# Seven-product matrix blocks: P3 ahead of P6, with P6's right block made by an accumulating DMA

## The chip, the core and the metric

The kernel runs on one core of a Trainium2 chip. The metric is the device time of one execution in microseconds. Five engines work side by side, each through its own queue in program order: TensorE (PE) multiplies and accumulates into banks of PSUM, VectorE (DVE) and ScalarE (ACT) do elementwise work and empty those banks, GpSimd (POOL) and SyncE (SP) here mostly issue DMAs. PE's weight loads are shown as an engine of their own (PEld).

## The reference

A trunk of two layers over 512 positions of width 1024, in float32. Each layer is half a SwiGLU mixer, a token mixer, and half a SwiGLU mixer again; layer 0 mixes tokens with a gated linear recurrence, layer 1 with a chunked spatial gate.

```python
def swiglu(x, w_in, w_out):
    g, u = jnp.split(x @ w_in, 2, axis=-1)
    return (jax.nn.silu(g) * u) @ w_out

for i in range(DEPTH):
    h = h + 0.5 * swiglu(rms_norm(h, ffn1_norm[i]), ffn1_w_in[i], ffn1_w_out[i])
    hn = rms_norm(h, mix_norm[i])
    ...
    h = h + m
    h = h + 0.5 * swiglu(rms_norm(h, ffn2_norm[i]), ffn2_w_in[i], ffn2_w_out[i])
return rms_norm(h, final_norm)
```

`w_in` is 1024 x 5632 and `w_out` 2816 x 1024 for each of the four SwiGLU mixers; the token mixers have a 1024 x 2048 input matrix and a 1024 x 1024 output matrix. Weights are read from device memory once or more; the work is almost wholly matrix products.

## The kernel before

**Precision.** Every float32 operand is split into a high and a low half of type fp32r: ACT rounds the value (`hi`, `whi`), DVE subtracts it from the original (`lo`, `wlo`). A product is three matmuls of 128x512 (lines 345 to 347): high by high, low by high, high by low.

**Seven products for eight.** A pair of 2x2 block matrices, left A and right B, is multiplied with seven block products (Winograd's form). The left sums are S1 = A21 - A22, S2 = S1 - A11, S4 = S2 + A12 and S3 = -S2 - A22. The products are taken in the order of `ORDER` (line 46):

| product | left (`LEFT`) | right | PSUM bank (`BANK`) |
|---|---|---|---|
| P1 | A11 | B11 | A, cleared |
| P2 | A12 | B21 | B, cleared |
| P5 | S1 | B11 + B12 | C, cleared |
| P6 | S2 | B11 + B12 + B22 | A, added to |
| P3 | S4 | B22 | C, added to |
| P7 | S3 | B12 + B22 | A, added to |
| Q4 | A22 | B11 + B12 + B21 + B22 | A, added to (`Q` of its own in output blocks) |

Each bank name stands for two PSUM banks, one for each of two halves `s` of the rows. Right after a product its `posts` entry reads the bank: it takes what has been summed in it so far, and the next product on that bank goes on adding to it. The post is ACT's or DVE's.

**Steps.** A product is done in two halves of its inner dimension, `ci` = 0 and 1, so one set of seven is 14 steps, each with a right block of 512 KB (two 128x512 tiles side by side) and 12 matmuls. In four of the output sets the first half is only one tile wide (256 KB, 6 matmuls). The main loop (line 1357) writes out, for step i: hooks of phase `pre`; the sum of step i+4, if it has one (`Sub.add`, line 1364); the split of step i+3 (`SPLIT_AHEAD`; `Sub.split`, ACT's `whi` and then DVE's `wlo`); hooks of phases `mid` and `rest`; new loads; the matmuls of step i, with the posts behind each row half. What is written out first stands first in an engine's queue. `whi` and `wlo` have four buffers each (line 59), so the split of step i+3 takes the buffers of step i-1 and cannot begin before that step's matmuls are done.

**Right blocks.** A `Raw` (line 111) is a weight block in one of eight buffers; SP loads it as soon as a buffer is free. Sums of weight blocks are made in two ways. `Raw.add` (line 136) issues a DMA from POOL's queue that adds another block from device memory onto the tile. `Sub.add` (line 163) sums two tiles on DVE and may then start an accumulating DMA onto the second tile (`tile_then`). `Sub.split` starts an accumulating DMA onto the tile it has just split, if the block has a `then` (line 184).

**Where sets stand.** `chunk` (line 624) makes 512 columns of gate and up products of a SwiGLU mixer, 20 sets in all; `out_blocks` (line 530) multiplies with `w_out` and adds into the residual `X`, 14 sets (one for each token mixer, three for each SwiGLU mixer, of which the first has the short first half); `seven_chunk` (line 1020) is one set in the spatial mixer. That is 35 sets, 70 halves. In a chunk the posts of P1, P5, P6 and P7 are ACT copies (`c<-A`, `c<-C`), those of P2 and P3 DVE operations. In an output set all posts are DVE's `upd` (line 545, `x<-A`, `x<-B`, `x<-C`). The token mixers' output sets do P1, P2, P5 of the first half, then of the second, then the rest product by product.

**Left sums.** `sums` (line 609) puts S2, S4 and S3 (DVE) on three successive steps; `Group.parts` splits them (`hi` on ACT, `lo` on DVE), in an output set at a place fixed by the product's position in the order (line 591). `BlockNorm.rest` does the same after a normalisation.

Of the kernel before, what the change touches and what calls it, by code (L numbers as in the profile page):

```python
# [11 lines left out]
ALU = mybir.AluOpType  # L12
# [30 lines left out]

ORDER = ("P1", "P2", "P5", "P6", "P3", "P7", "Q4")
LEFT = {"P1": "A11", "P2": "A12", "P5": "S1", "P6": "S2", "P3": "S4", "P7": "S3", "Q4": "A22"}
BANK = {"P1": ("A", True), "P2": ("B", True), "P5": ("C", True), "P6": ("A", False), "P3": ("C", False),
        "P7": ("A", False), "Q4": ("A", False)}
# [3 lines left out]
def trunk(ctx: ExitStack, tc: tile.TileContext, a: dict, out: bass.AP):  # L53
# [32 lines left out]
    def tt(o, x, y, op):  # L86
        nc.vector.tensor_tensor(out=o, in0=x, in1=y, op=op)  # L87
# [120 lines left out]
    def hook(n, phase, fn):  # L208


        hooks.setdefault((n, phase), []).append(fn)
# [106 lines left out]
    def seven(block, cuts, left, w, posts, order=None, own=False, apart=False, joined=None):  # L318

        bk, raw, held = {}, {}, []
        banks = dict(BANK, Q4=("Q", True)) if apart else BANK

        def mm_of(prod, ci):
            name, fresh = banks[prod]
            pairs = cuts[ci]

            def mm(sub):
                if fresh and ci == 0:
                    for s in range(2):
                        bk[name, s] = bank(name)[:, :w]
                if prod == joined and ci == 0:
                    held.extend((sub, q, i) for q, i in enumerate(pairs))
                    return
                for s in range(2):
                    ps = bk[name, s]
                    k = {} if fresh else dict(skip_group_check=True)  # L340
                    for sb, q, i in (held if prod == joined else []) + [(sub, q, i) for q, i in enumerate(pairs)]:
                        zh, zl = left(prod, i, s)
                        wh, wl = sb.hi[:, q, :], sb.lo[:, q, :]
                        end = i == cuts[-1][-1]
                        nc.tensor.matmul(ps, zh, wh, start=fresh and i == 0, stop=False, **k)  # L345
                        nc.tensor.matmul(ps, zl, wh, start=False, stop=False, **k)  # L346
                        nc.tensor.matmul(ps, zh, wl, start=False, stop=end, **k)  # L347
                    if ci == len(cuts) - 1 and prod in posts:
                        posts[prod](s, ps)
            return mm  # L350

        order = order or [(p, ci) for p in ORDER for ci in range(len(cuts))]
        for prod, ci in order:
            def new(k, n, plus=None):
                b = lambda k, n: block(k, n, cuts[ci])
                return raw_of(b(k, n), [P, len(cuts[ci]), w], plus and b(*plus))

            tile = then = tile_then = None
            if prod == "P1":
                r = raw[11, ci] = new(0, 0)  # L360
            elif prod == "P2":
                r = new(1, 0)
            elif prod == "P5":
                if own:
                    raw[11, ci] = new(0, 0, (0, 1))
                else:
                    tile = raw[12, ci] = new(0, 1)
                    tile_then = block(1, 1, cuts[ci])
                r = raw[11, ci]
            elif prod == "P6":  # L370
                r, tile, then = raw[11, ci], new(1, 1), block(1, 0, cuts[ci])
                raw[22, ci] = tile
            elif prod == "P3":
                r = raw[22, ci]
            elif prod == "P7":
                r = new(0, 1, (1, 1)) if own else raw[12, ci]
            else:
                r = raw[11, ci]
            subs.append(Sub(r, mm_of(prod, ci), None, tile, then, tile_then))
        return order  # L380
# [49 lines left out]
    class BlockNorm:  # L430
# [21 lines left out]
        def rest(self, n, a22=4):  # L452

            for i, g in enumerate(self.g):
                if a22 is not None:
                    hook(n + (9 if self.plain else a22), "mid", lambda g=g: g.parts("A22"))
                hook(n + 4 + i, "pre", g.s2)
                hook(n + 5 + i, "mid", lambda g=g: g.parts("S2"))
                n4, n3 = (n + 6 + i, n + 8 + i) if self.plain else (n + 7 + 2 * i, n + 10 + i)
                hook(n4, "pre", g.s4)  # L460
                hook(n4 + 1, "mid", lambda g=g: g.parts("S4", True))
                if self.plain:
                    hook(n3, "pre", lambda g=g: tt(g.new("A21"), g.f["S1"], g.f["A22"], ALU.add))
                    hook(n3 + 2, "mid", lambda g=g: g.parts("A21", True))
                hook(n3, "pre", g.s3)
                hook(n3 + 1, "mid", lambda g=g: (g.parts("S3", True), g.f.pop("S2")))
                hook(n3 + 1, "late", lambda g=g: g.f.pop("A22"))
# [62 lines left out]
    def out_blocks(w, k0, groups, scale, norm=None, order=None, own=False):  # L530

        n = [g for g in groups]
        cuts, bases, i, r = [], {}, 0, k0
# [11 lines left out]
        def upd(t, c, src, sc):  # L545
            stt(xt(t, c), src, sc, xt(t, c), ALU.mult, ALU.add)
# [15 lines left out]
        def p5(s, ps):  # L562
            upd(2 + s, 1, ps, scale)

        def p6(s, ps):
            upd(s, 1, ps, -scale)

        def p3(s, ps):
            upd(s, 1, ps, scale)
            final(s, 1, "A12", s)  # L570

        def p7(s, ps):
# [33 lines left out]
            g.stage(n + 1, "A21", src(0, 2))  # L606
            sums(g, n + 3)

    def sums(g, n):
        for i, fn in enumerate((g.s2, g.s4, g.s3)):  # L610
            hook(n + i, "pre", fn)

    def in_block(w, col, cw):
# [10 lines left out]
    def chunk(w_in, f0, nt, group):  # L624
# [18 lines left out]
        def p5(s, ps):  # L643
            act(new(c5, s, "c5"), ps, AF.Copy)

        def p6(s, ps):
            act(new(c2, s, "c2"), ps, AF.Copy)

        def p3(s, ps):
            tt(c2[s], ps, c2[s], ALU.subtract)  # L650
            stt(c2[s], c2[s], rt(s), c1[s], ALU.mult, ALU.mult)
            ht[s] = c2[s]
            if s == 1:
                left_blocks(group, ht, 0)
# [158 lines left out]
    def recurrent(w_in, w_out, norm):  # L813
# [169 lines left out]
        for c in range(KD):  # L983
            mk(c * P, lambda ps, c=c: y_post(c, ps), False)
        order = [(p, ci) for ci in range(2) for p in ("P1", "P2", "P5")]
        order += [(p, ci) for p in ("P6", "P3", "P7", "Q4") for ci in range(2)]
        gs = out_blocks(w_out, 0, [2, 2], 1.0, norm, order, own=True)
        gs.update(enumerate(groups))

# [1 line left out]
    def spatial(w_in, w_out, norm):  # L991
# [28 lines left out]
        def seven_chunk(base, done):  # L1020
# [11 lines left out]
                tt(c1[s], c1[s], ps, ALU.add)  # L1032
                soon(2 + s, s, 0, c1[s], c1[s])

            def p3(s, ps):
                tt(c2[s], ps, c2[s], ALU.subtract)
                soon(3 + s, s, 1, c2[s], c2[s])

            def p7(s, ps):
# [4 lines left out]
            def q4(s, ps):  # L1044
# [1 line left out]

            seven(in_block(w_in, lambda n: base + n * 512, 512), [[0, 1], [2, 3]], x_left(), 512,
                  dict(P1=lambda s, ps: copy(c1, s, ps, "c1"), P2=p2, P5=lambda s, ps: copy(c5, s, ps, "c5"),
                       P6=lambda s, ps: copy(c2, s, ps, "c2"), P3=p3, P7=p7, Q4=q4), own=True)

        def v_done(t, n, o, src):
            v[t, n] = o
# [116 lines left out]
        groups[1].stage(u0 + 9, "A12", lambda q, s: hts[1][s][:, (2 + q) * P : (3 + q) * P])  # L1169
        groups[1].stage(u0 + 10, "A22", lambda q, s: hts[1][2 + s][:, (2 + q) * P : (3 + q) * P], None, False)  # L1170
        groups[1].stage(u0 + 11, "A21", lambda q, s: hts[1][2 + s][:, q * P : (q + 1) * P])
        sums(groups[1], u0 + 13)
        order = [(p, ci) for ci in range(2) for p in ("P1", "P2", "P5")]
        order += [(p, ci) for p in ("P6", "P3", "P7", "Q4") for ci in range(2)]
        gs = out_blocks(w_out, 0, [2, 2], 1.0, norm, order, own=True)
        gs.update(enumerate(groups))

# [222 lines left out]
```

## Time and profile before

| what | value |
|---|---|
| median of three runs | 1653.03 us (1652.65 to 1653.19) |
| profiled execution | 1654.62 us, span 1652.9 us |
| PE busy | 1624.5 us, 98% of the span |
| DVE busy | 1373.8 us, 83% |
| ACT busy | 1034.6 us, 63% |
| POOL busy | 210.5 us, 13% |
| DMA traffic | 271.97 MB |

The profile is of one execution. "Busy" is the time in which an engine has an instruction under way; matmuls overlap in their pipeline, so their starts tell more than their durations. A row of the timeline has the start in us from the beginning of the span, the duration in us, engine, line of the kernel, operation, and the tiles out<-in with buffer numbers left out; in brackets stands idle time of the engine before it and what ended it. A window row has a stretch, its length, the busy time of each engine in it with instruction counts, the TensorE clock that was granted, the share of the DMA engines and GB/s. A row of DMA issues ends with the size and the median us from issue to landing.

### The profile page before, as it was taken

The numbers are of one execution on the slowest core, as the hardware profiler recorded it, in microseconds if no ns is written. First come the engines' busy times: TensorE is split into PE (matmuls) and PEld (weight loads), VectorE is DVE, ScalarE is ACT, GpSimd is POOL, SyncE is SP. The second block draws the span as 40 slices with busy tenths as digits, with TensorE's granted clock in tenths as the row PEclk, the third lists the DMA queues.
The fourth block names the chain that finished last, engine by engine and source line by source line (L and its number), as shares of the span: only waits on it lengthen the run. The fifth ranks groups of instructions, "written<-read, shape, count | busy, mean of one in ns | idle before, by whom it ended". The sixth has DMA issues, their size and how long they took to land.

```text
span 1652.9 us, 20807 instructions
## 1 busy us (share of the span) xinstructions
PE 1624.5 (98%) x7475; PEld 1336.9 (81%) x7475; DVE 1373.8 (83%) x1825; ACT 1034.6 (63%) x1487; POOL 210.5 (13%) x191
## 2 busy tenths in 40 slices
PE   8999999989999999999999999999999999999996
PEld 6788888878878888888888888888888888888885
DVE  5898897786798897887988978878966988879777
ACT  6656656666867656556676565566874765665655
POOL 1111111200010111111101111111200011121110
PEclk9999999999999999999999999999999999999998
DMA  6767876952463866976838778768863557696683
GB/s 205 158 174 175 208 165 153 218 140 77 102 148 92 195 164 162 217 182 155 203 96 182 173 163 208 185 161 202 218 172 90 151 119 188 166 209 168 157 206 77
DMA packets 160744, 271.97 MB, mean 165 GB/s; under 512 B 11280, under 2 KB 37504, under 8 KB 160640
## 3 DMA queue, kind: packets, MB, share of 16 engines
q1 hardware_dynamic: 113424, 181.95, 36.0%
q0 software_dynamic: 44992, 86.06, 31.1%
q10 hardware_dynamic: 2224, 2.63, 0.5%
q8 instruction: 59, 0.97, 0.2%
q14 instruction: 45, 0.37, 0.1%
HBM read 268.50 MB, written 2.10 MB: 164 GB/s over the span
## 4 chain that ended last, share of the span: by engine, by line
PE 86%; DVE 8%; ACT 4%; issue 2%; DMA 1%; SPq 0%; ACTq 0%; DVEq 0%
PE A L346 13%; PE A L347 13%; PE A L345 13%; PE C L346 7%; PE C L347 7%; PE C L345 7%; PE B L345 3%; PE B L347 3%; PE B L346 3%; PE e L260 3%; DVE wlo L87 2%; PE p L694 1%; PE p L692 1%; PE p L693 1%; PE Q L347 1%
## 5 line engine op out<-in xcount | busy, mean ns | idle before, releaser
L96 ACT ACTIVATE whi<-raw 128x1024 fp32r<-128x1024 f32 (+1 forms) x539 | 556.4, 1034 | 421.4 <-PE A L346 107.4
L87 DVE TENSOR_TENSOR wlo<-raw,whi 128x1024 fp32r<-128x1024 f32 (+1 forms) x539 | 640.5, 1191 | 198.3 <-ACT whi L96 197.4
L345 PE MATMUL A<-whi,hi 128*128 128x512 f32 x984 | 393.0, 399 | 0.0
L346 PE MATMUL A<-whi,lo 128*128 128x512 f32 x984 | 385.5, 392 | 2.5 <-DVE lo L87 2.4
L347 PE MATMUL A<-wlo,hi 128*128 128x512 f32 x984 | 385.5, 392 | 0.2 <-DVE wlo L87 0.2
L346 PEld LDWEIGHTS A<-whi,lo 128*128 128x128 f32 x984 | 185.8, 189 | 41.7 <-DVE lo L87 4.8
L347 PEld LDWEIGHTS A<-wlo,hi 128*128 128x128 f32 x984 | 185.4, 188 | 40.8 <-DVE wlo L87 0.6
L345 PEld LDWEIGHTS A<-whi,hi 128*128 128x128 f32 x984 | 185.7, 189 | 36.5
L346 PE MATMUL C<-whi,lo 128*128 128x512 f32 x544 | 212.4, 390 | 0.9 <-DVE lo L87 0.7
L345 PE MATMUL C<-whi,hi 128*128 128x512 f32 x544 | 212.3, 390 | 0.0
L347 PE MATMUL C<-wlo,hi 128*128 128x512 f32 x544 | 211.8, 389 | 0.0
L136 POOL DMA_DIRECT2D raw<-in_ffn_w_in_dram x80 | 96.4, 1205 | 757.4 <-DVE raw L87 591.2
L87 DVE TENSOR_TENSOR raw<-raw,raw 128x1024 f32<-128x1024 f32 (+1 forms) x118 | 141.6, 1200 | 0.5
L87 DVE TENSOR_TENSOR lo<-a,hi 128x512 fp32r<-128x512 f32 (+1 forms) x196 | 127.8, 659 | 11.2 <-ACT hi L96 10.9
L136 POOL DMA_DIRECT2D raw<-in_ffn_w_out_dram x72 | 83.0, 1153 | 385.0 <-DMA raw<-in_ffn_w_out_dram 137.0
L346 PEld LDWEIGHTS C<-whi,lo 128*128 128x128 f32 x544 | 102.1, 188 | 24.1 <-DVE lo L87 3.2
L96 ACT ACTIVATE hi<-a 128x512 fp32r<-128x512 f32 (+1 forms) x196 | 117.4, 601 | 6.2 <-DVE a L87 4.0
L345 PEld LDWEIGHTS C<-whi,hi 128*128 128x128 f32 x544 | 102.1, 188 | 21.5 <-ACT c L96 0.4
L347 PEld LDWEIGHTS C<-wlo,hi 128*128 128x128 f32 x544 | 102.1, 188 | 21.0
L96 ACT ACTIVATE c<-A 128x512 f32<-128x512 f32 x126 | 74.1, 595 | 56.6 <-PE A L347 56.2
L345 PE MATMUL B<-whi,hi 128*128 128x512 f32 x272 | 109.2, 401 | 0.0
L347 PE MATMUL B<-wlo,hi 128*128 128x512 f32 x272 | 106.3, 391 | 0.0
(165 smaller groups left out, 2193.4 us busy)
## 6 DMA issues: line engine op xcount, KB each, us to landing
raw<-in_ffn_w_in_dram SPq DMA_DIRECT2D x160, 512.0 KB, 4.5
raw<-in_ffn_w_out_dram SPq DMA_DIRECT2D x100, 512.0 KB, 5.4
raw<-in_ffn_w_in_dram POOLq DMA_DIRECT2D x80, 512.0 KB, 7.6
raw<-in_ffn_w_out_dram POOLq DMA_DIRECT2D x60, 512.0 KB, 7.9
raw<-in_sg_w_in_dram SPq DMA_DIRECT2D x18, 512.0 KB, 5.0
raw<-in_rec_w_in_dram SPq DMA_DIRECT2D x16, 512.0 KB, 3.9
raw<-in_ffn_w_in_dram SPq DMA_DIRECT2D x30, 256.0 KB, 3.9
raw<-in_ffn_w_out_dram SPq DMA_DIRECT2D x20, 256.0 KB, 4.1
```

Of the source, the lines that this page charges most:

```text
L87: nc.vector.tensor_tensor(out=o, in0=x, in1=y, op=op)
L96: nc.scalar.activation(out=o, in_=x, func=f, **k)
L136: nc.gpsimd.dma_start(out=self.v, in_=src, accum_op=ALU.add)
L260: nc.tensor.transpose(ps[:, o : o + P], src(q, s), ident)
L345: nc.tensor.matmul(ps, zh, wh, start=fresh and i == 0, stop=False, **k)
L346: nc.tensor.matmul(ps, zl, wh, start=False, stop=False, **k)
L347: nc.tensor.matmul(ps, zh, wl, start=False, stop=end, **k)
L692: nc.tensor.matmul(ps, zh, wh, start=start and q == 0, stop=False)
L693: nc.tensor.matmul(ps, zl, wh, start=False, stop=False)
L694: nc.tensor.matmul(ps, zh, wl, start=False, stop=stop and q == 1)
```

## The change

P3 now stands ahead of P6 in all 35 sets. P6's right block B11 + B12 + B22 is no longer summed on DVE from P5's tile and a loaded B22: when P5's tile (B11 + B12) has been split, an accumulating DMA from POOL's queue adds B22 to it. B22 is still loaded for P3. In all, 70 DVE sums of 128x1024 leave, and 70 accumulating DMAs come; the number of plain loads, of matmuls and of ACT instructions is the same. Q4's block still gets its last term, B21, from an accumulating DMA after P6's split, which now stands two steps later. The banks keep their products, so P3 adds to C right after P5, and P7 adds to A right after P6. The posts of the two products are exchanged with them (c2 = P3, then c2 - P6), and S4 is made earlier and split ahead of S2's split.

```diff
-ORDER = ("P1", "P2", "P5", "P6", "P3", "P7", "Q4")
+ORDER = ("P1", "P2", "P5", "P3", "P6", "P7", "Q4")
...
                     tile_then = block(1, 1, cuts[ci])
-                r = raw[11, ci]
+                r, then = raw[11, ci], block(1, 1, cuts[ci])
             elif prod == "P6":
-                r, tile, then = raw[11, ci], new(1, 1), block(1, 0, cuts[ci])
-                raw[22, ci] = tile
+                r, then = raw[11, ci], block(1, 0, cuts[ci])
             elif prod == "P3":
-                r = raw[22, ci]
+                r = new(1, 1)
...
-                hook(n + 5 + i, "mid", lambda g=g: g.parts("S2"))
-                n4, n3 = (n + 6 + i, n + 8 + i) if self.plain else (n + 7 + 2 * i, n + 10 + i)
+                n4, n2, n3 = (n + 5 + i, n + 7 + i, n + 8 + i) if self.plain else (n + 6 + i, n + 8 + 2 * i, n + 10 + i)
+                hook(n2, "mid", lambda g=g: g.parts("S2"))
...
+        def p3(s, ps):
+            upd(s, 1, ps, scale)
+
         def p6(s, ps):
             upd(s, 1, ps, -scale)
-
-        def p3(s, ps):
-            upd(s, 1, ps, scale)
             final(s, 1, "A12", s)
...
-    def sums(g, n):
-        for i, fn in enumerate((g.s2, g.s4, g.s3)):
+    def sums(g, n, after=(0, 1, 2)):
+        for i, fn in zip(after, (g.s2, g.s4, g.s3)):
             hook(n + i, "pre", fn)
...
+        def p3(s, ps):
+            act(new(c2, s, "c2"), ps, AF.Copy)
+
         def p6(s, ps):
-            act(new(c2, s, "c2"), ps, AF.Copy)
-
-        def p3(s, ps):
-            tt(c2[s], ps, c2[s], ALU.subtract)
+            tt(c2[s], c2[s], ps, ALU.subtract)
             stt(c2[s], c2[s], rt(s), c1[s], ALU.mult, ALU.mult)
...
-        order += [(p, ci) for p in ("P6", "P3", "P7", "Q4") for ci in range(2)]
+        order += [(p, ci) for p in ("P3", "P6", "P7", "Q4") for ci in range(2)]
...
-            def p3(s, ps):
-                tt(c2[s], ps, c2[s], ALU.subtract)
+            def p6(s, ps):
+                tt(c2[s], c2[s], ps, ALU.subtract)
                 soon(3 + s, s, 1, c2[s], c2[s])
...
-                       P6=lambda s, ps: copy(c2, s, ps, "c2"), P3=p3, P7=p7, Q4=q4), own=True)
+                       P3=lambda s, ps: copy(c2, s, ps, "c2"), P6=p6, P7=p7, Q4=q4), own=True)
...
-        sums(groups[1], u0 + 13)
+        sums(groups[1], u0 + 13, (0, 0, 1))
```

More of the change, by code (lines that the diff above doesn't have):

```diff
@@ L1171, in spatial @@
         groups[1].stage(u0 + 11, "A21", lambda q, s: hts[1][2 + s][:, q * P : (q + 1) * P])
-        sums(groups[1], u0 + 13)
+        sums(groups[1], u0 + 13, (0, 0, 1))
         order = [(p, ci) for ci in range(2) for p in ("P1", "P2", "P5")]
-        order += [(p, ci) for p in ("P6", "P3", "P7", "Q4") for ci in range(2)]
+        order += [(p, ci) for p in ("P3", "P6", "P7", "Q4") for ci in range(2)]
         gs = out_blocks(w_out, 0, [2, 2], 1.0, norm, order, own=True)
```

## The prediction

> **What bounds the kernel now.** I read the page first: shares of the engines, DMA queues, the costly groups. Then the windows, to see where PE is idle at all.
>
> ```profile
> PE 1624.5 (98%) x7475; PEld 1336.9 (81%) x7475; DVE 1373.8 (83%) x1825; ACT 1034.6 (63%) x1487; POOL 210.5 (13%) x191
> ...
> q1 hardware_dynamic: 113424, 181.95, 36.0%
> q0 software_dynamic: 44992, 86.06, 31.1%
> ...
> L87 DVE TENSOR_TENSOR raw<-raw,raw 128x1024 f32<-128x1024 f32 (+1 forms) x118 | 141.6, 1200 | 0.5
> ```
>
> ```profile
> 0.00:150.00 150.00, 143.34 (x622) 113.42 (x623) 120.24 (x183) 92.86 (x145) 21.32 (x29) 0.98 0.71 183
> 150.00:300.00 150.00, 150.00 (x682) 124.03 (x681) 125.40 (x166) 88.12 (x110) 24.84 (x23) 1.00 0.75 176
> 300.00:450.00 150.00, 144.79 (x736) 122.27 (x735) 116.98 (x169) 105.69 (x164) 8.42 (x7) 0.99 0.50 123
> 1500.00:1653.00 153.00, 139.33 (x628) 114.57 (x626) 123.40 (x167) 86.25 (x121) 16.87 (x14) 0.97 0.63 152
> ```
>
> PE is the bound: 28.4 us of the span of 1652.9 are without a matmul, and 6.7, 5.2 and 13.7 of them lie in the three stretches with the opening, the first stage border and the tail. Elsewhere PE hardly stops. So the change can win a few us, and can lose wherever it makes PE wait. It touches PE in one way: each PSUM bank must have been read by the post of one product before the next product may add to it. Before, P5 (bank C) was followed by P6 on A, and P3 came back to C two steps later; P6 (A) was followed by P3 on C, and P7 came back to A two steps later. Now P5 and P3 stand back to back on C, and P6 and P7 on A. What decides is how soon the posts come.
>
> The next rows are the timeline around the border after P5 in a chunk: PE's last matmul on C and first on A, ACT's queue, DVE's split of P5's first half, POOL's two transfers onto P7's tiles. Behind them stand DMA rows of short windows: the first of these two transfers, the second, and P6's two (issued 166.05 and 169.06).
>
> ```profile
> 169.67 0.39 PE L347 MATMUL C<-wlo,hi 128*128 128x512 f32 x1
> 169.90 0.39 PE L345 MATMUL A<-whi,hi 128*128 128x512 f32 x1
> 167.70 1.04 ACT L96 ACTIVATE whi<-raw 128x1024 fp32r<-128x1024 f32 x1
> 168.74 0.60 ACT L96 ACTIVATE c<-C 128x512 f32<-128x512 f32 x1
> 170.10 0.60 ACT L96 ACTIVATE c<-C 128x512 f32<-128x512 f32 x1 [0.76 <-PE C L347]
> 157.67 1.22 DVE L87 TENSOR_TENSOR wlo<-raw,whi 128x1024 fp32r<-128x1024 f32 x1
> 155.94 1.20 POOL L136 DMA_DIRECT2D raw<-in_ffn_w_in_dram  x1 [24.65 <-DVE raw L87]
> 158.28 1.20 POOL L136 DMA_DIRECT2D raw<-in_ffn_w_in_dram  x1 [1.14 <-ACT c L96]
> ...
> raw<-in_ffn_w_in_dram POOLq DMA_DIRECT2D x1, 512.0 KB, 8.6
> raw<-in_ffn_w_in_dram POOLq DMA_DIRECT2D x1, 512.0 KB, 8.8
> raw<-in_ffn_w_in_dram POOLq DMA_DIRECT2D x2, 512.0 KB, 6.5
> ```
>
> Matmul starts are 0.23 us apart, so a step of 12 is 2.72 us. ACT reads C's first half until 169.34, and PE leaves P5 at 169.90: a margin of 0.56 us. The `whi` ahead of that copy is the split three steps ahead: before, P3's first half; after, **P6's first half, which needs the new transfer**.
>
> **Part 1: 70 sums leave DVE.** 70 of the 118 sums of 1.2 us are 84 us of DVE's 1373.8. On the path they are worth only the stalls that DVE causes there. PE's idle time outside the three stretches is 28.4 - 25.6 = 2.8 us, and the borders in them hold a little more: I take a gain of 5 us, at most 10.
>
> **Part 2: 70 accumulating DMAs come.** POOL spends 1.20 us on each issue, 84 us more on an engine that is busy for 13%: no cost in itself. DMA time: 86.06 MB of accumulating transfers are 164 of 512 KB, and take 31.1% of the 16 engines, so 3.1 us each; 70 of them (35 MB) raise the two queues' share from 67% to 80%. A mean of 80% does not bind, but the place does. In a chunk POOL's queue now holds, in order: P7's first half, P7's second, the new one for P6's first half, the new one for the second. The rows: P7's two are issued 2.34 us apart and land at 164.54 and 167.08, 2.54 apart. P5's `wlo` ends at 158.89 and POOL is free at 159.48, so the third goes out at about 159.5. If it lands 2.54 after the one ahead, that is 169.6. The `whi` that could start at 167.70 then runs 169.6 to 170.65, the copy of C to 171.25, and PE, which wants C at 169.90, waits 1.35 us. Bounds: a transfer with the queue to itself (6.5 us, P6's row) lands at 166.0, and there is no wait; and loads share the engines. B22's buffer comes free two steps earlier than before, so the next set's load falls into this stretch; 181.95 MB are 347 loads of 512 KB in 36.0% of the span, 1.7 us each. One whole load ahead makes it 171.3, a wait of 3.05. I take a quarter of a load, 1.75 us, being nearest to the back-to-back rows, for 21 sets (20 chunks, one spatial): 37 us.
>
> On the order in one queue the Trainium skill, "DMA: Bandwidth & Descriptors", section "Queues, rings and completion order", says that on each DMA engine descriptors are consumed in ring order; the two landings 2.54 us apart agree.
>
> In an **output set** the post after P5 is DVE's, behind `wlo` and a `lo` of the same step. Rows: PE's border, ACT's `whi`, DVE's queue, and the two transfers onto P7's tiles there (both, then the first alone).
>
> ```profile
> 209.74 0.39 PE L347 MATMUL C<-wlo,hi 128*128 128x512 f32 x1
> 209.97 0.39 PE L345 MATMUL A<-whi,hi 128*128 128x512 f32 x1
> 207.27 1.06 ACT L96 ACTIVATE whi<-raw 128x1024 fp32r<-128x1024 f32 x1 [0.81 <-ACT hi L96]
> 210.09 1.22 DVE L87 TENSOR_TENSOR wlo<-raw,whi 128x1024 fp32r<-128x1024 f32 x1
> 211.23 0.69 DVE L87 TENSOR_TENSOR lo<-a,hi 128x512 fp32r<-128x512 f32 x1
> 211.91 1.28 DVE L93 SCALAR_TENSOR_TENSOR x<-C,x 128x512 f32<-128x512 f32 x2
> 195.40 2.48 POOL L136 DMA_DIRECT2D raw<-in_ffn_w_out_dram  x2 [11.37 <-DMA raw<-in_ffn_w_out_dram]
> ...
> raw<-in_ffn_w_out_dram POOLq DMA_DIRECT2D x2, 512.0 KB, 8.0
> raw<-in_ffn_w_out_dram POOLq DMA_DIRECT2D x1, 512.0 KB, 7.4
> ```
>
> C's first half is read until 212.55, 2.6 us after PE would want it; today nobody cares. DVE is behind there: ACT's `whi` ended at 208.33, `wlo` began at 210.09. Two sums (2.4 us) leave ahead of this place, so DVE should then be held by ACT: `wlo` at 208.33, the post 1.14 + 0.68 later by the starts in the rows, and 0.64 for one: 210.8, still 0.85 us late. That is the floor with the transfer in time. With the transfer: P7's second is issued 1.24 after 195.40 and lands 8.6 later (twice 8.0 less 7.4), at 205.2; plus 2.5 is 207.7, `whi` starts 0.45 late, and the wait is 1.3. With a whole load, 3.0. I take a quarter of a load again, 1.7 us, for 14 sets: 24 us.
>
> **Part 3: P7 right behind P6.** Rows: DVE's reading of P3's banks, whose place in the queues P6's post takes, and PE's start of P7, in the same chunk and output set.
>
> ```profile
> 180.35 0.68 DVE L87 TENSOR_TENSOR c<-C,c 128x512 f32<-128x512 f32 x1
> 180.78 0.39 PE L345 MATMUL A<-whi,hi 128*128 128x512 f32 x1
> 221.55 1.28 DVE L93 SCALAR_TENSOR_TENSOR x<-C,x 128x512 f32<-128x512 f32 x2
> 220.84 0.39 PE L345 MATMUL A<-whi,hi 128*128 128x512 f32 x1
> ```
>
> In the chunk the bank is read until 181.03, 0.25 us after P7 wants it: 21 x 0.25 = 5 us. In the output set until 222.19, 1.35 us late with DVE behind, 0.85 by the floor above: I take 0.9, since PE's first wait lets DVE catch up; 14 x 0.9 = 13 us. The second half of each bank has six matmuls (1.36 us) of cover, and I cost it at nothing; where the post of the second half came later than that, it would add what is over.
>
> **Part 4: Q4's last term two steps later.** P6's transfer had six steps (16.3 us) to Q4's split and now has four (10.9 us), less about 2.6 for `whi`, `wlo` and issue: 8.3 us. It lands after 6.5 (its row): covered, by 1.8 us. If it took 8.8, as P7's do, 0.5 us of wait would come on each of 35 sets. S4 made one step earlier stays three steps ahead of its matmuls: nothing.
>
> **Part 5: the clock.** Windows with a PE pause and what follows it, and the matmuls that end the two pauses.
>
> ```profile
> 355.10:356.40 1.30, 0.39 (x2) 0.19 (x2) 1.30 (x3) 1.06 (x4) 0.00 (x0) 1.00 0.01 2
> 356.40:359.80 3.40, 3.40 (x26) 3.40 (x27) 3.40 (x8) 2.58 (x5) 0.00 (x0) 1.00 0.54 157
> 462.20:464.60 2.40, 0.30 (x2) 0.00 (x0) 2.40 (x7) 2.07 (x4) 0.00 (x0) 1.00 0.87 169
> 465.00:468.40 3.40, 3.40 (x10) 2.62 (x9) 3.40 (x7) 0.00 (x0) 1.18 (x1) 0.50 0.72 96
> ...
> 356.39 0.39 PE L219 MATMUL r<-zl,whi 128*128 128x256 f32 x1 [0.91 <-DVE zl L93]
> 464.67 0.50 PE L346 MATMUL A<-whi,lo 128*128 128x512 f32 x1 [2.17 <-DVE lo L87]
> ```
>
> A pause of 0.91 us left the clock at 1.00; one of 2.17 was followed by 3.4 us at 0.50, which costs 1.7 us more. The waits I expect lie between. I let a fifth of the 35 sets pay: 12 us; the ends are none and 60. The Trainium skill, "TensorE: Matmul & The Clock Gate", Part 1, has the clock go down after an idle window of about 3.4 us; by that these waits would cost no clock and the sum would lack its 12 us, but the pause of 2.17 us here did cost it.
>
> **Sum.** 37 + 24 + 5 + 13 + 12 - 5 = 86 us on the profiled 1654.6 us: 1740.6; the median of the runs is 1.6 lower, so about 1738 us, 5% slower.
>
> **The rivals.**
>
> *The transfers come in time.* Then only the floors are left: 21 x 0.25 + 14 x (0.85 + 0.9) - 5 = 25 us, 1678. For it: alone a transfer takes 6.5, and 159.5 + 6.5 is before 167.70. Against: three in a row, each pair in the rows 2.4 to 2.5 apart. It needs a landing within 8.7 us of issue (by 168.2).
>
> On its side is the Trainium skill, "DMA: Bandwidth & Descriptors", section "Anatomy of one DMA": its fit of 2.0 us and the bytes over 436e3 would be an estimated 3.2 us for 512 KB. The rows have 6.5 to 8.8.
>
> *The clock goes down in every set.* Whole loads ahead of the transfers, 21 x (3.05 + 0.25) + 14 x (3.0 + 1.35) = 130, plus 60 of clock, less 5: about 1838. For it: loads and transfers share the 16 engines, and a wait of 3 us is past the 2.17. Against: a longer set leaves DMA more time.
>
> *Faster: DVE's relief decides.* In the output sets the posts come behind DVE's backlog; with 2.4 us of sums gone they could all end before PE asks. It needs the transfer by 168.2 in chunks, and the post by 209.97 in output sets, 0.85 us earlier than the queue behind `whi` allows by the rows. Then the gain of 5 is alone: 1648.
>
> *Nothing to be seen* (within 0.2%, 3.3 us, about what runs of this kernel can tell): waits and relief cancel at some 5 us each, 1653.
>
> **How the numbers follow.** Chances: the forecast (1700 to 1790) 0.53, transfers in time (1660 to 1700) 0.24, clock in every set (1790 to 1850) 0.15, faster 0.05, same 0.03. So slower 0.92. The range 1670 to 1810 leaves out the last two, the low end of the second and the greater part of the third, near 2 in 10.
>
> **What the profile after would show.** PE idle before `C<-whi,hi` put down to ACT `c` in chunks and DVE `x` in output sets, 1.5 to 2 us a set; smaller waits before `A<-whi,hi` on DVE `c` and `x`; ACT `whi` waiting for a DMA onto `raw`, in tens of us; windows with the clock at 0.50 inside sets; `raw<-raw,raw` down to 48 and POOL's issues up by 70. The prediction is wrong if ACT's `whi` shows no such wait for DMA, or if PE idles on something other than banks A and C.

## The result and the profile after

The changed kernel takes 1789.44 us (median of six runs, 1785.63 to 1799.86) against 1653.14 us for the kernel before beside it (1652.65 to 1654.51): a ratio of 1.0833, 95% interval 1.0813 to 1.0852. The prediction said slower, 1738 us, 1670 to 1810: the sign and the range held, and 51 of the 136 us were missing from its sum. The profiled execution took 1785.63 us, with a span of 1783.8, which is 130.9 us longer than the span before.

The first fence is the page of the changed kernel: engines, DMA queues, the chain that ended last, and three groups, with idle time and its cause behind the bar.

```profile
PE 1660.0 (93%) x7475; PEld 1347.3 (76%) x7475; DVE 1307.4 (73%) x1755; ACT 1034.5 (58%) x1487; POOL 293.8 (16%) x261
...
q0 software_dynamic: 63520, 121.71, 40.2%
...
PE 48%; DMA 21%; DVE 15%; ACT 8%; issue 6%; POOL 2%; SPq 0%; POOLq 0%; ACTq 0%; DVEq 0%
...
L345 PE MATMUL A<-whi,hi 128*128 128x512 f32 x984 | 394.3, 401 | 15.5 <-DVE x L93 10.3
...
L345 PE MATMUL C<-whi,hi 128*128 128x512 f32 x544 | 227.8, 419 | 84.8 <-ACT c L96 51.6
```

DVE lost 66 us of work and gained nothing by it: it is now 73% busy, waiting like the rest. DMA holds 21% of the chain that ended last. Before, the group onto C had no idle time at all; now PE idles 84.8 us ahead of it and 15.5 us ahead of the group onto A. The list of waits of the changed kernel (total us, times, longest) says for what:

```profile
ACT whi L96 <- DMA raw<-in_ffn_w_in_dram: 129.0, 47, 7.9
...
PE C L345 <- ACT c L96: 51.6, 21, 6.9
...
ACT whi L96 <- DMA raw<-in_ffn_w_out_dram: 45.1, 21, 5.3
...
PE C L345 <- DVE x L93: 33.2, 14, 4.4
...
PE A L345 <- DVE x L93: 10.3, 14, 1.5
...
PE A L345 <- DVE c L87: 5.2, 21, 1.8
```

One wait before C and one before A in each of the 35 sets, ACT's `c` in the 21 chunk and spatial sets, DVE's `x` in the 14 output sets. How one comes about shows in the timeline of the changed kernel: first an ordinary chunk (POOL, ACT, PE), then the first chunk behind an output set with the short first half, then an output set.

```profile
685.69 2.44 POOL L136 DMA_DIRECT2D raw<-in_ffn_w_in_dram  x2 [1.07 <-ACT c L96]
697.73 1.06 ACT L96 ACTIVATE whi<-raw 128x1024 fp32r<-128x1024 f32 x1 [3.47 <-DMA raw<-in_ffn_w_in_dram]
698.69 1.07 ACT L96 ACTIVATE c<-C 128x512 f32<-128x512 f32 x2
699.32 0.50 PE L345 MATMUL C<-whi,hi 128*128 128x512 f32 x1 [1.77 <-ACT c L96]
...
640.70 3.68 POOL L136 DMA_DIRECT2D raw<-in_ffn_w_in_dram  x3 [1.07 <-ACT c L96]
653.57 1.06 ACT L96 ACTIVATE whi<-raw 128x1024 fp32r<-128x1024 f32 x1 [6.20 <-DMA raw<-in_ffn_w_in_dram]
655.17 0.61 PE L345 MATMUL C<-whi,hi 128*128 128x512 f32 x1 [4.50 <-ACT c L96]
...
737.86 1.06 ACT L96 ACTIVATE whi<-raw 128x1024 fp32r<-128x1024 f32 x1 [1.74 <-DMA raw<-in_ffn_w_out_dram]
738.95 1.23 DVE L87 TENSOR_TENSOR wlo<-raw,whi 128x1024 fp32r<-128x1024 f32 x1 [0.61 <-ACT whi L96]
740.09 0.68 DVE L87 TENSOR_TENSOR lo<-a,hi 128x512 fp32r<-128x512 f32 x1
740.69 1.28 DVE L93 SCALAR_TENSOR_TENSOR x<-C,x 128x512 f32<-128x512 f32 x2
741.52 0.47 PE L345 MATMUL C<-whi,hi 128*128 128x512 f32 x1 [1.41 <-DVE x L93]
```

Read the first four rows backwards. PE stood still for 1.77 us until the copy of C had read the first half; the copy stood in ACT's queue behind `whi`; `whi` had waited 3.47 us for a transfer, the second of the two issued from 685.69. In the next three rows three transfers went out in one go from 640.70, some 2 us later against PE than in an ordinary set, and PE waited 4.50. In the output set two DVE instructions stand between the late `whi` and the post.

### The profile page after: what moved, and what is told of

It is laid out like the page before. It is cut to its first block, busy times and chain, and to the rows that moved or that the text cites. A ratio compares the mean times of both kernels' runs of the same rounds, so it can differ in the third digit from the quotient of the medians.

```text
span 1783.8 us, 20898 instructions
## 1 busy us (share of the span) xinstructions
PE 1660.0 (93%) x7475; PEld 1347.3 (76%) x7475; DVE 1307.4 (73%) x1755; ACT 1034.5 (58%) x1487; POOL 293.8 (16%) x261
## 3 DMA queue, kind: packets, MB, share of 16 engines
q0 software_dynamic: 63520, 121.71, 40.2%
## 4 chain that ended last, share of the span: by engine, by line
PE 48%; DMA 21%; DVE 15%; ACT 8%; issue 6%; POOL 2%; SPq 0%; POOLq 0%; ACTq 0%; DVEq 0%
DMA raw<-in_ffn_w_in_dram 11%; DMA raw<-in_ffn_w_out_dram 8%; PE A L345 7%; PE A L346 7%; PE A L347 6%; DVE wlo L87 5%; PE C L345 5%; ACT whi L96 5%; PE C L346 4%; PE C L347 4%; DVE x L93 2%; DVE lo L87 2%; DVE raw L87 2%; PE e L260 2%; POOL raw L136 2%
## 5 line engine op out<-in xcount | busy, mean ns | idle before, releaser
L345 PE MATMUL A<-whi,hi 128*128 128x512 f32 x984 | 394.3, 401 | 15.5 <-DVE x L93 10.3
L345 PE MATMUL C<-whi,hi 128*128 128x512 f32 x544 | 227.8, 419 | 84.8 <-ACT c L96 51.6
L136 POOL DMA_DIRECT2D raw<-in_ffn_w_in_dram x120 | 145.3, 1263 | 811.0 <-DVE raw L87 489.5
L346 PE MATMUL C<-whi,lo 128*128 128x512 f32 x544 | 222.7, 409 | 0.0
L347 PE MATMUL C<-wlo,hi 128*128 128x512 f32 x544 | 221.8, 408 | 0.0
L345 PEld LDWEIGHTS C<-whi,hi 128*128 128x128 f32 x544 | 108.6, 200 | 121.1 <-ACT c L96 60.5
L136 POOL DMA_DIRECT2D raw<-in_ffn_w_out_dram x96 | 111.1, 1176 | 374.3 <-DMA raw<-in_ffn_w_out_dram 161.4
L347 PEld LDWEIGHTS C<-wlo,hi 128*128 128x128 f32 x544 | 108.8, 200 | 24.5
L346 PEld LDWEIGHTS C<-whi,lo 128*128 128x128 f32 x544 | 108.8, 200 | 22.1
L96 ACT ACTIVATE hi<-a 128x512 fp32r<-128x512 f32 (+1 forms) x196 | 117.0, 601 | 12.6 <-DVE a L87 10.3
L346 PE MATMUL B<-whi,lo 128*128 128x512 f32 x272 | 106.1, 390 | 0.0
L93 DVE SCALAR_TENSOR_TENSOR x<-A,x 128x512 f32<-128x512 f32 x112 | 71.9, 684 | 7.4 <-PE A L347 7.3
```

The source lines that it names most:

```text
L93: nc.vector.scalar_tensor_tensor(out=o, in0=x, scalar=s, in1=y, op0=op0, op1=op1)
L96: nc.scalar.activation(out=o, in_=x, func=f, **k)
L136: nc.gpsimd.dma_start(out=self.v, in_=src, accum_op=ALU.add)
```

## The experiments

Each time is the median of its runs; "over before" is against the kernel before on the same chip, beside a ratio with its 95% interval.

**1. Take the late transfer away.** P5's tile gets no B22, so P6's block is whole as soon as P5's is.

```diff
-                r, then = raw[11, ci], block(1, 1, cuts[ci])
+                r = raw[11, ci]
```

> The changed kernel without the 70 new transfers and without a sum in their place: B22 is left out of P6's right block, and so out of Q4's. Theory 1 (the transfer lands late, and its lateness reaches PE through the post that bank C waits for): the waits before P3 fall to nothing in chunks and to 0.85 us in output sets, those before P7 stay at 0.33 and 0.9; about 1678 us. Rival (banks used back to back cost this much by themselves): the waits before P3 stay near 2.6 us a set, above 1750 us.

Measured: 1702.62 us, 51 over before (1.0305, 1.0290 to 1.0320). So the transfers cost 85 us of the 136, and the floor without them is twice the 25 us that the prediction gave to its rival "the transfers come in time". Waits and three pauses of this run:

```profile
PE C L345 <- DVE x L93: 19.3, 14, 2.7
...
PE A L345 <- DVE x L93: 10.0, 14, 1.6
...
PE C L345 <- ACT c L96: 5.9, 2, 3.8
PE A L345 <- DVE c L87: 5.1, 21, 1.9
```

```profile
99.38 0.47 PE L345 MATMUL C<-whi,hi 128*128 128x512 f32 x1 [1.93 <-DVE x L93]
...
216.71 0.47 PE L345 MATMUL C<-whi,hi 128*128 128x512 f32 x1 [0.90 <-DVE x L93]
...
339.61 0.76 PE L345 MATMUL C<-whi,hi 128*128 128x512 f32 x1 [2.45 <-DVE x L93]
```

The chunks are rid of their waits before C: 2 are left of 21. In the output sets the floor is there: 0.90 at 216.71, which is the set that the prediction took its 0.85 from; but a set with the short first half (99.38) stands at 1.93, and the one ahead of the first token mixer (339.61) at 2.45. The mean is 1.38 (19.3 in 14).

**2. The order alone.** P6's block comes from a sum on DVE again, as before.

```diff
-                r, then = raw[11, ci], block(1, 0, cuts[ci])
+                r, tile, then = raw[11, ci], raw[22, ci], block(1, 0, cuts[ci])
...
-                r = new(1, 1)
+                r = raw[22, ci] = new(1, 1)
```

> The new order alone: P3 ahead of P6, but P6's right block is summed on DVE from P5's tile and P3's, as before. Theory 1: no wait of ACT for a transfer; chunks wait under 0.5 us before P3, but output sets wait about 2.5 us before P3 and 1.3 before P7, since DVE is behind by the two sums: about 1653 + 14 x 3.8 + 21 x 0.5 = 1717 us. Rival (DVE's relief is worth nothing at these banks): within 5 us of the run without transfers and sums.

Measured: 1768.58 us, 117 over before (1.0703, 1.0685 to 1.0721). The sums cost 66 us on top of experiment 1, where the two expectations are 39 apart. A wait of ACT and a group of PE:

```profile
ACT whi L96 <- DMA raw<-in_ffn_w_in_dram: 58.7, 26, 3.9
```

```profile
L345 PE MATMUL C<-whi,hi 128*128 128x512 f32 x544 | 225.5, 415 | 58.1 <-DVE x L93 29.3 <-ACT hi L96 14.2 <-ACT c L96 9.5
```

Of the 58.1 us before C, 48.6 lie in the 14 output sets, 3.5 each where 2.5 were expected. And I expected no wait of ACT for a transfer: there are 26, all but two of them for Q4's last term, which goes out after P6's late split. The expectation also had no term for the clock, which is at 0.50 in 18 stretches here. In this place DVE's sum costs somewhat less than the DMA that replaced it (66 us against 85 on top of experiment 1).

**3. Give P3 a bank of its own.** P3 starts afresh on B, which is free there.

```diff
-BANK = {"P1": ("A", True), "P2": ("B", True), "P5": ("C", True), "P6": ("A", False), "P3": ("C", False),
+BANK = {"P1": ("A", True), "P2": ("B", True), "P5": ("C", True), "P6": ("A", False), "P3": ("B", True),
...
-                if fresh and ci == 0:
+                if fresh and ci == 0 and prod != "P3":
```

> The changed kernel with all its transfers, but P3 starts afresh on bank B, which P2's post has read two steps before, and leaves out the sum with P5. Theory 1: ACT still waits some 170 us for transfers, but PE no longer waits before P3; left are the 21 us before P7: 1665 to 1685 us. Rival (PE waits for late operands, or the DMA engines are simply full): PE loses the time elsewhere, above 1740 us.

Measured: 1753.57 us, 102 over before (1.0616, 1.0600 to 1.0632). My theory fell here. The waits before P3 are gone, as they had to be, and the time is not. Waits of this run:

```profile
ACT whi L96 <- DMA raw<-in_ffn_w_in_dram: 177.9, 66, 6.8
...
PE A L345 <- DVE c L87: 31.2, 21, 4.1
...
PE A L345 <- DVE x L93: 24.3, 10, 3.6
```

The wait before A, 15.5 us in the changed kernel, is now 63.1, of which the last two rows hold 55.5. PE runs on through P3, and arrives at P7, the next product that follows its own bank, with ACT and DVE as late as before.

**4. Send the new transfer ahead.** P7's transfers go out two steps later in chunks and three in output sets, so that P6's are ahead of them in POOL's queue.

```diff
-                pending.append((now[0] + 2, self))
+                pending.append((now[0] + self.lag, self))
...
-                self.tile.add(self.tile_then)
+                hook(now[0] + 2, "late", lambda t=self.tile, b=self.tile_then: t.add(b))
...
+                if own:
+                    r.lag = 5
```

> The changed kernel with P7's accumulating transfers issued later (in chunks two steps later, in output sets three), so that the new transfers are no longer behind them in POOL's queue. Same number of transfers. If the new transfer is late because it stands behind P7's two in one queue: it lands 6 to 8 us after issue instead of 10 to 11, chunks wait under 0.5 us before P3, output sets about 1 us: 1680 to 1700 us. Rival (the loads and the sheer amount of transfers make it late): it still lands after 9.5 us or more, above 1750 us.

Measured: 1766.82 us, 115 over before (1.0697, 1.0655 to 1.0739). In this kernel the matmul of high by high stands on line 347:

```profile
ACT whi L96 <- DMA raw<-in_ffn_w_in_dram: 133.5, 77, 3.4
```

```profile
PE A L347 <- DVE c L87: 47.9, 21, 3.8
PE C L347 <- DVE x L93: 18.7, 13, 3.3
...
PE C L347 <- ACT c L96: 5.9, 2, 3.8
```

The transfer for P6 is in time in the chunks (ACT's `c` before C: 5.9 us in 2, not 51.6 in 21), and P7's and Q4's are late instead: 77 waits of ACT for DMA, and 47.9 us of PE before A. The delay can be handed on from one transfer to the next; it is not used up.

**5. Free both banks.** P3 on B and P7 on C, both afresh.

```diff
-BANK = {"P1": ("A", True), "P2": ("B", True), "P5": ("C", True), "P6": ("A", False), "P3": ("C", False),
-        "P7": ("A", False), "Q4": ("A", False)}
+BANK = {"P1": ("A", True), "P2": ("B", True), "P5": ("C", True), "P6": ("A", False), "P3": ("B", True),
+        "P7": ("C", True), "Q4": ("A", False)}
...
-                if fresh and ci == 0:
+                if fresh and ci == 0 and prod not in ("P3", "P7"):
```

> The changed kernel with all its transfers, but P3 starts afresh on bank B and P7 afresh on bank C, and both leave out what those banks held; so no product adds to a bank right after another, except Q4 after P7's old place on A. If PE's loss comes about at the back-to-back banks, and a late transfer costs only there: 1653 to 1670 us, though ACT still waits over 100 us for transfers. Rival (late transfers reach PE in any case, or take its operands): above 1700 us.

Measured: 1725.61 us, 73 over before (1.0443, 1.0416 to 1.0470). No product waits before A or C for a post now, and yet:

```profile
ACT whi L96 <- DMA raw<-in_ffn_w_in_dram: 196.0, 70, 8.7
...
PE e L260 <- DVE c L93: 22.5, 24, 2.3
```

DVE's product `c`, which PE transposes after the chunk (`e<-ident,c`), stands in DVE's queue behind late `wlo`. That row is the largest of PE's waits, not all of them: PE idles 78.5 us in this run against 28.4 before, and most of the rest is spread over late halves of operands (`lo`, `wlo`, `whi`, `hi`). So late blocks reach PE in more ways than over the two banks.

**6. The order alone with both banks free.** The edit of experiment 5 in the kernel of experiment 2. Against experiment 2:

```diff
-        "P7": ("A", False), "Q4": ("A", False)}
+        "P7": ("C", True), "Q4": ("A", False)}
...
-                if fresh and ci == 0:
+                if fresh and ci == 0 and prod not in ("P3", "P7"):
```

> The order alone with the sums on DVE, as in the run of the order alone, but P3 starts afresh on bank B and P7 on bank C (leaving out what these held). If the 117 us of the order alone were the back-to-back banks: within 10 us of the kernel before, 1645 to 1663. Rival (the new order itself brings operands or left sums late): above 1700 us.

Measured: 1692.41 us, 39 over before (1.0238, 1.0222 to 1.0254), again above what I expected. ACT's splits wait 70.2 us for blocks of `w_in`, 30 times, though P6's block needs no transfer here: all but two of these waits are for Q4's last term.

**7. Neither transfers nor sums, both banks free.** The edit of experiment 1 in the kernel of experiment 5. Against experiment 5:

```diff
-                r, then = raw[11, ci], block(1, 1, cuts[ci])
+                r = raw[11, ci]
```

> The new order with P3 made afresh on bank B and P7 afresh on bank C (so no product adds to a bank right behind the one that was there), and with neither the 70 new transfers nor the 70 sums on DVE. Left out: B22 from P6's right block, and the sums that P3 and P7 should have taken over from P5 and P6, so that those posts read other values of the same size. Theory: the new order costs only through its banks, and what was left in the run with both banks freed (73 us over the kernel before) came from the late transfers. Then nothing is left to wait for and DVE has 84 us less to do: 1645 to 1665 us. Rival: the order has a cost of its own that is neither bank nor transfer (P7 and Q4 each need a transfer within fewer steps, the left sums stand nearer to their use): 1685 us or more, with ACT's splits of Q4 and P7 waiting for DMA.

Measured: 1653.96 us, 1.3 over before (1.0014, 1.0005 to 1.0024). The first line below is of its page, the others are its waits.

```profile
PE 1619.5 (98%) x7475; PEld 1334.8 (81%) x7475; DVE 1301.8 (79%) x1755; ACT 1033.8 (63%) x1487; POOL 209.7 (13%) x191
```

```profile
ACT whi L96 <- DMA raw<-in_ffn_w_out_dram: 24.8, 6, 5.2
...
ACT whi L96 <- DMA raw<-in_ffn_w_in_dram: 12.0, 7, 2.6
```

The order and the 70 sums less on DVE together cost nothing and win nothing; an order that costs a few us and a relief that wins as many would look the same here. With experiments 1, 2, 5 and 6 this makes a table of the time over before, in us:

| P6's block is made by | banks as in the change | both banks free |
|---|---|---|
| nothing (B22 left out) | 51 | 1 |
| a sum on DVE | 117 | 39 |
| an accumulating DMA | 136 | 73 |

Two causes, each of which costs alone, over the 1 us without either: products back to back on a bank 50 us, late blocks 72. Together they cost 135, 13 more than their sum.

**8. The same transfers, read by nobody.** The kernel before, with 70 accumulating DMAs of the same blocks, issued at the same splits, onto two spare tiles (`SLOTS` 58 instead of 60 makes room).

```diff
+            if self.spare is not None:
+                src, i = self.spare
+                nc.gpsimd.dma_start(out=scr[i][:, : k * c].rearrange("p (k c) -> p k c", k=k), in_=src, accum_op=ALU.add)
             if self.then is not None:
...
+            if prod == "P5":
+                subs[-1].spare = block(1, 1, cuts[ci]), ci
```

> The kernel before, unchanged in order, banks and sums, with 70 accumulating transfers more, of the same weight blocks at the same places in POOL's queue, but onto two spare tiles that nobody reads. Theory: the volume alone is not the price, since the loads and transfers of the kernel before have slack; what costs is that someone needs the landing at once. Then 1653 to 1670 us. Rival: the 35 MB more delay the loads and the transfers that the other products need: over 1690 us, with ACT's splits waiting for DMA in tens of us and no waits before C.

Measured: 1655.73 us, 3.1 over before (1.0018, 1.0008 to 1.0027). A row of its page:

```profile
q0 software_dynamic: 63520, 121.71, 41.7%
```

The same 121.71 MB as in the changed kernel, in less time, for 3 us. So the volume alone is not what costs; what the changed kernel has beside it is that someone needs these landings at once.

**9. The chunks alone.** Order and transfers changed in the 20 chunks only. Against the kernel before, beside the order and the posts:

```diff
-                r = raw[11, ci]
+                r = raw[11, ci]
+                if not own:
+                    then = block(1, 1, cuts[ci])
-            elif prod == "P6":
+            elif prod == "P6" and not own:
+                r, then = raw[11, ci], block(1, 0, cuts[ci])
+            elif prod == "P3" and not own:
+                r = new(1, 1)
+            elif prod == "P6":
```

> The change made in the 20 chunks alone; output sets and the spatial set stay as before. By the trace of the change the chunks' share is 52 us before P3, 6.5 before P7 and some 12 of clock: 1710 to 1730 us. If the chunks suffer only because the output sets before them are late: under 1690.

Measured: 1733.68 us, 81 over before (1.0486, 1.0472 to 1.0501), a little above the range.

**10. The other sets alone.** The 14 output sets and the spatial set.

```diff
-                r = raw[11, ci]
+                r = raw[11, ci]
+                if own:
+                    then = block(1, 1, cuts[ci])
-            elif prod == "P6":
+            elif prod == "P6" and own:
+                r, then = raw[11, ci], block(1, 0, cuts[ci])
+            elif prod == "P3" and own:
+                r = new(1, 1)
+            elif prod == "P6":
```

> The change in the 14 output sets and the spatial set alone (30 of the 70 transfers, 30 sums fewer); the 20 chunks as in the kernel before. The run with the chunks alone was 81 us over the kernel before, the whole change 136 us. Theory: the sets cost what they cost each by themselves, so the rest of 55 us is theirs: 1700 to 1715 us, with PE's idle time before P3's first matmul in every output set near 2.5 us. The prediction's own terms for these sets (24 for P3, 13 for P7, 2 for the spatial set, 5 of the clock) give 1695. Rival: the output sets are late mainly because the chunks ahead of them are (full queue, DVE behind): then the sum of the two parts falls short of the whole, 1685 us or less.

Measured: 1716.93 us, 64 over before (1.0388, 1.0371 to 1.0406). Against my 55: 81 and 64 are 145, and the whole change costs 136, so each kind of set pays for itself. Why the sum is 9 more than the whole is not shown; a pause in one set may let the queues of the next catch up. Apart from the spatial set's 4.1, the output sets' idle time before P3 is 32.2 us, 2.3 a set, near the 2.5 expected. The group onto C in the chunks' run and, below, in this one:

```profile
L345 PE MATMUL C<-whi,hi 128*128 128x512 f32 x544 | 220.2, 405 | 55.4 <-ACT c L96 55.4
```

```profile
L345 PE MATMUL C<-whi,hi 128*128 128x512 f32 x544 | 219.3, 403 | 36.3 <-DVE x L93 26.7 <-ACT whi L96 5.4 <-ACT c L96 4.1
```

**11. The same transfers with products kept apart.** In the chunks P1, P5, P2, P6, P3, P7, Q4: P5 goes ahead, P6's block is made by the same 40 DMAs, one product still lies between P5 and P6, but now neither P3 nor P7 follows right on its own bank.

```diff
+              [(p, ci) for p in ("P1", "P5", "P2", "P6", "P3", "P7", "Q4") for ci in range(2)])
```

> As the run with chunks alone, with the same 40 transfers and the same 40 sums gone, but the chunks' products in the order P1, P5, P2, P6, P3, P7, Q4: P6's transfer still has four steps, and no two products on one bank stand together but P7 and Q4, as before. If the back-to-back banks are the cause and DVE's relief is worth a little: 1643 to 1656 us, at or below the kernel before. Rival (the transfers themselves cost): above 1670 us.

Measured: 1664.26 us, 11 over before (1.0069, 1.0056 to 1.0081), where the chunks of the change cost 81 with as many transfers. Its waits, and its group onto C:

```profile
ACT whi L96 <- DMA raw<-in_ffn_w_in_dram: 87.9, 40, 7.6
```

```profile
L345 PE MATMUL C<-whi,hi 128*128 128x512 f32 x544 | 213.8, 393 | 0.0
```

ACT still waits 87.9 us for DMA, and PE never before C. Here Q4's last term has its old six steps too, so this run does not tell the banks from that.

**12. That, with P7's transfers issued four steps later.**

```diff
-                self.tile.add(self.tile_then)
+                hook(now[0] + 4, "late", lambda t=self.tile, b=self.tile_then: t.add(b))
```

> In the 20 chunks the order P1, P5, P2, P6, P3, P7, Q4 with the 40 new transfers (everything else as before), as in the earlier run at 1664 us, but with P7's two transfers issued four steps later, so that the ones that P6 waits for go out ahead of them. Theory: the 11 us that were left there are ACT's waits for P6's transfer (80 us of ACT's time, some 8 us on PE), and a free queue takes them away while DVE keeps its relief: 1645 to 1656 us. Rival: P7's transfers are late in their turn, as they were when the same was tried with the order of the change: 1664 us or more, with the idle time of PE before P7's matmuls.

Measured: 1665.32 us, 13 over before (1.0079, 1.0065 to 1.0092). It won nothing. ACT's waits for these blocks fall from 87.9 to 58.3 us, and the idle time before P7 that the rival names does not come either; but PE now waits 10.8 us before `e`, behind DVE's `c`, against 3.6 in experiment 11. No version tried is faster than the kernel before.

## Why the prediction was right, and where it was too low

**The mechanism held in the changed kernel.** What idle time PE has gained lies ahead of banks C and A, put down to the engines that were named, one wait on each in every set; ACT's `whi` waits 129 and 45 us for DMA onto `raw`, where tens were forecast; the sums are down to 48. Experiment 8 bears out "a mean of 80% does not bind, but the place does".

**The terms**, as forecast and as the profile after has them (idle time of PE):

| term of the sum | forecast | measured |
|---|---|---|
| before P3, chunks and spatial (Part 2) | 37 | 51.6 |
| before P3, output sets (Part 2) | 24 | 33.2 |
| before P7, chunks and spatial (Part 3) | 5 | 5.2 |
| before P7, output sets (Part 3) | 13 | 10.3 |
| the clock (Part 5) | 12 | 23 |
| PE's restart after each of 70 pauses | not in it | 11 |
| PE's other idle time (relief of DVE, Part 1) | -5 | -5 |
| not found | | 1 |
| sum | 86 | 131 (span) |

The clock's 23 is the excess of the matmul starts of lines 345 to 347 over 0.227 us a start, in stretches with a granted clock under 0.9 and without the starts that end a pause: 26.0 us against 2.9 before. The restart is that the first start after a pause comes 0.16 us later than the idle time alone gives: at these 70 places 127.3 us lie between starts, of which 100.3 are idle and 15.9 are 70 ordinary distances. PE's other idle time went from 28.4 to 23.5 us. That fits the relief, but may as well come of the pauses, in which DVE catches up: in experiment 7, with the sums gone and no such pauses, PE idles 31.6 us.

One agreement is luck. The 20 chunks wait 0.17 us each before P7, not 0.25, and the spatial set alone waits 1.85; that makes the 5.2.

**The step that failed is the size of Part 2's wait**, 61 forecast and 84.8 measured. In the chunks the failure is one of sampling. The quarter of a load was a good choice for the chunk it was read from (1.63 us there against 1.75), and 16 ordinary chunks wait 1.6 us each (25.4 in all). But the other four wait 23.1 together, 5.8 each: the first chunk of all, most of whose wait stays without the transfers (3.8 in experiment 1), and three of the four that follow an output set with the short first half, where, as in the rows at 640.70, the transfers start later.

In the output sets both parts of the size were off. The floor of 0.85 was right where it was read (0.90 in experiment 1), and the seven sets of that kind average 0.7 there. The other seven, those with a short first half and those in or just ahead of a token mixer, average 2.05. With the transfer both kinds wait alike, 2.40 and 2.34 us, against 1.7: to the ordinary ones the transfer adds 1.7, twice what was forecast, to the others 0.3. I read one set of each kind and multiplied.

**What the sum could not show.** The prediction says that the change touches PE in one way, over the banks. Experiments 3 and 5 refute that as an account of the cause: with the waits before C removed they come before A, and with both removed 73 us remain. The banks were only the first place where a late ACT and DVE met PE. Part 4's "covered, 0" therefore held in the changed kernel only beside the other waits; with both banks free, DVE's `c` at the chunk's end is late. Q4's last term is late in such kernels: in experiments 2 and 6 it ends 24 and 28 of ACT's waits, before none, and in experiment 7, where P6's split has nothing to wait for, 5. So four steps cover it only while P6's split is on time. That it is what makes `c` late is argued, and no run shows it alone.

**The rivals.** Transfers in time, at 1678, would have been 1702.6 by experiment 1. The clock went down in 17 stretches ahead of the tail (4 before), not in every set. That DVE's relief decides is refuted by the result, and experiment 7, where the relief is whole and PE waits before neither bank, is 1.3 us slower, not faster.

## What to carry to other kernels

In this kernel, whose first engine is 98% busy, an operand's lateness was not paid where the operand is used, but at the next place where that engine needed something from the queues which the lateness held up; removing that place moved part of the payment on (136 us with both banks, 102 with one freed, 73 with both). Before pricing a border, list the kinds of stages that have it, and read one row of each kind, the ones next to an irregular stage above all; and a floor read from the kernel before does not say what the new transfer adds to it. Taking work off an engine that is not the bound was worth nothing here, and the DMA that replaced it cost by how soon its landing was needed, not by its bytes.

## What was not expected of the hardware

**The clock goes by how much of a pause falls into one step of a grid.** The trace of the changed kernel has 18 stretches with a granted clock of 0.50. All begin on one grid of 3.413 us, and each lasts one or more whole steps of it. The window rows are cut by that grid: for each of three pauses of PE the step or steps with the pause, and the step behind the first and the third (PE's busy time is the number behind the length, the granted clock the third from the end). Two of the pauses stand below, the third, of 1.77 us, at 699.32 further up.

```profile
136.57:139.99 3.42, 1.64 (x8) 1.05 (x7) 1.18 (x2) 2.03 (x3) 0.00 (x0) 1.00 1.10 263
139.99:143.40 3.41, 3.41 (x10) 2.66 (x9) 0.77 (x3) 1.06 (x1) 1.20 (x1) 0.50 0.85 193
221.91:225.32 3.41, 2.37 (x11) 1.63 (x9) 2.12 (x5) 1.58 (x2) 0.00 (x0) 1.00 1.09 268
225.32:228.74 3.42, 2.20 (x10) 1.86 (x11) 2.54 (x5) 1.58 (x2) 1.22 (x1) 1.00 0.70 190
696.37:699.78 3.41, 1.64 (x8) 1.06 (x7) 0.96 (x1) 2.03 (x3) 0.00 (x0) 1.00 1.10 261
699.78:703.19 3.41, 3.41 (x17) 2.80 (x16) 0.69 (x2) 1.52 (x2) 1.20 (x1) 1.00 0.83 195
```

```profile
139.31 0.50 PE L345 MATMUL C<-whi,hi 128*128 128x512 f32 x1 [1.78 <-ACT c L96]
...
226.54 0.47 PE L345 MATMUL C<-whi,hi 128*128 128x512 f32 x1 [2.26 <-DVE x L93]
```

The pause of 1.78 us lies in one step, and the next step runs at 0.50. The pause of 2.26 us is longer, but the grid cuts it into 1.04 and 1.22, and no clock is lost. The pause of 1.77 us lies in one step and just misses. So it is in all of this run: PE was idle for 1.78 us or more in the step ahead of each of the 22 steps at 0.50, and for no more than that ahead of any other. In experiment 4 up to 1.95 us of idle time in a step passed without loss, so the border is not the same in every run. Part 5's pauses of 0.91 and 2.17 us therefore could not say how many sets would pay. The Trainium skill, "TensorE: Matmul & The Clock Gate", Part 1, has the clock drop after an idle window of about 3.4 us and calls that window free-running. The length agrees with the grid here; that a whole window must be idle does not, since little more than half of one was enough.

**A transfer lands the later, the more stand ahead of it in its queue.** DMA rows of short windows of the changed kernel, in the chunk at 694: P7's second block, that one with P6's first (the median of the two), and P6's second.

```profile
raw<-in_ffn_w_in_dram POOLq DMA_DIRECT2D x1, 512.0 KB, 8.7
raw<-in_ffn_w_in_dram POOLq DMA_DIRECT2D x2, 512.0 KB, 9.9
raw<-in_ffn_w_in_dram POOLq DMA_DIRECT2D x1, 512.0 KB, 12.3
```

P6's first block needs about 11 us from issue to landing (twice 9.9 less 8.7), where one with the queue to itself took 6.5 before. The fit in the Trainium skill, "DMA: Bandwidth & Descriptors", section "Anatomy of one DMA", which gives an estimated 3.2 us, has no term for what stands ahead in the queue, and is far from these.
